# Writing the fp32r high part of h from PSUM on ScalarE, in a hybrid diffusion step on one Trainium2 core

## The chip, the core and the metric

The kernel runs on one core of one Trainium2 chip, as a single launch. The metric is the device time of one execution in microseconds (us); a run is given as the median of several executions. Engine names in the rows: PE is TensorE's matmul stream, PEld its weight loads, DVE is VectorE, ACT is ScalarE, POOL is GpSimd, SP is SyncE, which issues the DMAs.

## The reference

One step of a backbone over 2048 latent tokens and 128 prompt tokens, of width 1024. What bears on the change is the head of the layer: a root-mean-square norm, a scale and a shift per channel that come from the conditioning vector, and one combined projection whose columns feed four branches.

```python
def trunk_layer(x, cond, S0, ada_w, ada_b, norm_g, w_in, ...):
    mod = jax.nn.silu(cond) @ ada_w + ada_b
    shift, scale, gate = jnp.split(mod, 3, axis=-1)
    h = rmsnorm(x, norm_g) * (1 + scale[:, None]) + shift[:, None]
    p = h @ w_in
    qkv, g_a, beta_logit, a_logit, uv, g_b, x_c, g_c, x_d, g_d = jnp.split(p, _split_points(), axis=-1)
    y_a, S_new = deltanet_branch(qkv, g_a, beta_logit, a_logit, S0, conv_qkv, a_log, dt_bias, dn_norm_g)
    y_b = sgu_branch(uv, g_b, sgu_norm_g, sgu_w, sgu_b)
    y_c = pool_branch(x_c, g_c, pool_w, pool_scale)
    y_d = fourier_branch(x_d, g_d, fourier_w)
    out = jnp.concatenate([y_a, y_b, y_c, y_d], axis=-1) @ w_out
    return x + gate[:, None] * out, S_new
```

The first branch is a chunked gated delta rule: in chunks of 64 tokens it needs the inverse of a unit lower triangular matrix per chunk and head (`triangular_solve` in the reference), and then a scan over the chunks in both directions.

## The kernel before, in words

**Tiles and groups.** The latent tokens are 16 tiles of 128, the prompt is one more. They go through the first phase in three groups (`phase_a(gi)`, gi = 0, 1, 2). The transposed, modulated activations of one group stand in `hT`: the channels on the partitions, in 8 feature blocks f of 128 channels, the group's tokens on the free axis, 776 columns for groups 0 and 1 (six tiles and 8 columns of the next for the convolution), 640 for group 2. `hT` has one copy only. So a block of it may be written for the next group when the last projection of the old group has read it.

**Two parts of fp32.** The projections run in fp32r on TensorE, with each fp32 operand split in a high part (its rounding to fp32r) and a low part (the rest). `hT[0]` holds the high parts, `hT[1]` the low ones. `mm3` (L246 to L250) issues three matmuls for each feature block: high by high, high by low, low by high. Weights are loaded and split in the same way by `load_w` (L229 to L244): high part on ScalarE (L242) or, later in the program, on VectorE (L240), low part by a subtract on VectorE or GpSimd (L243).

**From x to hT.** `x_prep` loads tiles of x, adds the position embedding, and scales each token by its reciprocal root mean square (L331, in place). `x_fin` (L334) goes over the 8 feature blocks. For each: up to four TensorE transposes (L342) into one bank of PSUM `ps`; one ScalarE activation with the scale and bias of the block's channels, which writes the fp32 tile `h` (L344; four buffers, shared with another use under the tag "pr"); then `h_split`: VectorE's cast of `h` to fp32r, which is the high part (L353), and the subtract of the two, which is the low part (L354), on VectorE for even f and on GpSimd for odd f. Where `spill` is set, SyncE then stores `h` to DRAM (L348). The bank is one of two (`pa`) for the first half of group 0, taken in turn from `pc` and `pa` for its second half, and the single bank `pc` for groups 1 and 2. There are 56 such blocks: 24 of 384 columns, 16 of 392, and 16 of 128 (tile 15 and the prompt, in group 2).

**What follows in a group.** The first projection gives x_d and the delta-rule logits (272 columns per tile of tokens; matmuls at L250 named `pj<-BIG 128x272`; evicted by ScalarE into `xdt`, L923, and by VectorE into `lg`, L924). Then, for each of two pairs of heads, the convolution channels k, q and v are projected (chunks of 384 and 392 columns), convolved on VectorE (L832) and turned to token order. `pair_pre` builds the chunk matrices: key products (matmuls L660), decay factors (exp on ScalarE for Pd, Po and Pf, the last at L681), products on VectorE (Ld at L670, Po at L676, Pf at L692 with the matmuls L690). Pair 1's `pair_pre` of groups 0 and 1 is held back (`pend`) and runs after the next group's x_d projection. When both pairs are there, `lanes_solve` (L728, L730) inverts the triangular blocks step by step, VectorE and GpSimd each on its share of the rows; for group 0 it is cut into five pieces that are pulled in between other work, and groups 1 and 2 are solved together. Later come the scan, the Fourier branch, the other branches and the output projection with the residual (in the trace from about 1040 us on).

**What sets the order.** No order is written by hand. Each engine has one queue that runs in order; a scheduler fills the queues from the program's order, its priorities and its own estimate of when things are ready. So an edit in one place can move instructions on every engine. `x_prep` and `x_fin` run under one raised priority (`hp(OXv[0])`), `load_w` under another, and the projections' matmuls under none.

Of the kernel before, what the change touches and what calls it, by code (L numbers as in the profile page):

```python
# [9 lines left out]
F32 = mybir.dt.float32  # L10
# [3 lines left out]
AF = mybir.ActivationFunctionType  # L14
ALU = mybir.AluOpType
# [129 lines left out]
def tile_dit_step(ctx: ExitStack, tc: tile.TileContext, io: dict, dbg=None, stop=None):  # L145
    nc = tc.nc
# [53 lines left out]
    hT = [BIG[:, i * NH:(i + 1) * NH].rearrange("p (k t) -> p k t", k=KC) for i in range(2)]  # L200
# [6 lines left out]
    modab = cst.tile([128, 2, KC, 2], F32, name="modab")  # L207
# [5 lines left out]
    def hp(o):  # L213
        return tc.high_priority(offset=o)
# [119 lines left out]
    def x_fin(prep, fs=range(KC), pss=(pc,)):  # L334
        with hp(OXv[0]):
            tiles, off, spill, xts = prep
            w = sum(rows for _, rows in tiles)
            cond = 1 if tiles[0][0] == NTS else 0
            for f in fs:
                ps = pss[f % len(pss)]()  # L340
                for j, (i, rows) in enumerate(tiles):
                    nc.tensor.transpose(ps[:, j * 128:j * 128 + rows], xts[j][:rows, f * 128:(f + 1) * 128], ident[:rows, :rows])  # L342
                h = hp_.tile([128, 512], F32, tag="pr", name="h", bufs=4)
                nc.scalar.activation(h[:, :w], ps[:, :w], AF.Identity, scale=modab[:, 0, f, cond:cond + 1],  # L344
                                     bias=modab[:, 1, f, cond:cond + 1])
                h_split(h[:, :w], f, off)
                if spill is not None:
                    nc.sync.dma_start(out=h_d[spill, :, f, off:off + 384], in_=h[:, :384])  # L348

    def h_split(h, f, off):  # L350
        w = h.shape[1]
        hi = hT[0][:, f, off:off + w]
        nc.vector.tensor_copy(hi, h)  # L353
        (nc.gpsimd if f % 2 else nc.vector).tensor_tensor(hT[1][:, f, off:off + w], h, hi.bitcast(F32), op=ALU.subtract)  # L354

    def out_dbg(name, ap):
        if name in dbg:
# [4 lines left out]
    with tc.tile_pool(name="ada", bufs=3, reuse_waits="tile") as ada_p:  # L362
# [82 lines left out]
        with hp(300):  # L445
            mod_q(0, a0)
        a2 = ada_load(2)
        x_fin(p1, (0, 1), (pa,))
        with hp(300):
            mod_q(1, a1)  # L450
        a3 = ada_load(3)
        xd_k(range(3), 0)
        x_fin(p1, (2, 3), (pa,))
        with hp(300):
            mod_q(2, a2)
        xd_k(range(3), 1)
        x_fin(p1, (4, 5), (pa,))
        with hp(300):
            mod_q(3, a3)
# [866 lines left out]
    op = [ctx.enter_context(tc.tile_pool(name="opa_", bufs=1, side="right", reuse_waits="tile"))]  # L1326
# [110 lines left out]
```

## Time and profile before

| | |
|---|---|
| median of 3 runs | 1256.94 us (1252.34 to 1257.28) |
| the profiled execution | 1259.96 us |
| its span on the core | 1258.2 us |
| granted TensorE clock, mean | 0.917 |
| busy in the span: PE, DVE, ACT, POOL | 1100.5, 875.8, 414.3, 560.2 us |
| DMA | 204.21 MB, 162 GB/s mean |

The profiled execution is one program run, 1.8 us longer than its span, and 3.0 us above the median. Times in the rows below are us from the span's start. The busy shares are averages over stages that differ, so the rows are cut by stretch. The granted clock is the share of TensorE's full speed that was granted in the stretch; 1.00 is 2.4 GHz, and the lower level is 1.2 GHz.

### The profile page before, as it was taken

To read this page: it belongs to the slowest core of one execution; us is meant where nothing else is said; L and a number is where in the kernel's file an instruction comes from. 1 tells how busy PE (TensorE), PEld (TensorE's weight loads), DVE (VectorE), ACT (ScalarE), POOL (GpSimd) and SP (SyncE) were. 2 spreads that over 40 slices of the span, in tenths; PEclk is the share of its full clock that TensorE was granted. 3 is DMA by queue.
4 is the path that set the end of the run, shared out by engine and by line. 5 is a ranking of instruction groups with operands and counts; after the bars stand their busy time and mean duration, and the time that the engine had idled before them with its cause. 6 is when DMAs were issued, how large, how long until landed. Compare 5 with 4: busy or idle time off the path is not lost.

```text
span 1258.2 us, 28860 instructions
## 1 busy us (share of the span) xinstructions
PE 1100.5 (87%) x11635; PEld 998.4 (79%) x11635; DVE 875.8 (70%) x1864; ACT 414.3 (33%) x836; POOL 560.2 (45%) x551
## 2 busy tenths in 40 slices
PE   5798999986578899878997989999899979999997
PEld 2598888875566889774886878888889969999997
DVE  3768886999987477999577263584433378888665
ACT  2355765444344585310523102112111211111111
POOL 1347456799973154797040033223132543432212
PEclk9999988998766899798998989999999969999999
DMA  9978559543271558425245656767735555544331
GB/s 303 331 265 269 148 136 254 189 102 72 60 169 40 128 129 188 111 82 189 61 122 164 168 149 180 232 211 253 208 119 177 176 169 164 174 144 140 122 126 68
DMA packets 251388, 204.21 MB, mean 162 GB/s; under 512 B 109138, under 2 KB 218706, under 8 KB 250998
## 3 DMA queue, kind: packets, MB, share of 16 engines
q1 hardware_dynamic: 251254, 202.37, 55.1%
q8 instruction: 91, 1.49, 0.5%
q14 instruction: 43, 0.35, 0.1%
HBM read 138.86 MB, written 63.46 MB: 161 GB/s over the span
## 4 chain that ended last, share of the span: by engine, by line
PE 35%; DVE 8%; DMA 7%; POOL 5%; issue 3%; SPq 2%; ACT 1%; DVEq 0%; POOLq 0%; ACTq 0%
PE pj L250 28%; DMA wst<-in_wt_dram 3%; PE pa L1043 3%; POOL LL L730 2%; POOL ltmp L728 2%; DVE BIG L240 1%; DMA tab<-in_cdft_dram 1%; DVE X L752 1%; POOL BIG L243 1%; PE pb L1384 1%; PE pc L1043 1%; SPq L1034 1%; DMA ga<-ga_d 1%; DMA wos<-in_wo_dram 1%; DVE BIG L1207 1%
## 5 line engine op out<-in xcount | busy, mean ns | idle before, releaser
L250 PE MATMUL pj<-BIG 128*128 128x256 f32 (+4 forms) x3888 | 638.6, 320 | 34.0 <-DVE BIG L240 7.8
L250 PEld LDWEIGHTS pj<-BIG 128*128 128x128 f32 x3888 | 581.2, 201 | 54.9 <-issue 13.9
L250 PE MATMUL pj<-BIG,yh 128*128 128x256 f32 x1088 | 196.9, 287 | 5.7 <-ACT BIG L1346 4.7
L250 PEld LDWEIGHTS pj<-BIG,yh 128*128 128x128 f32 x1088 | 164.8, 191 | 8.8 <-ACT BIG L1346 5.1
L243 POOL TENSOR_TENSOR BIG<-wst,BIG 128x512 fp32r<-128x512 f32 (+1 forms) x66 | 94.7, 1436 | 171.9 <-DVE BIG L240 77.7
L250 PE MATMUL pj<-BIG,yl 128*128 128x256 f32 x544 | 141.9, 286 | 0.0
L250 PEld LDWEIGHTS pj<-BIG,yl 128*128 128x128 f32 x544 | 99.0, 191 | 0.7
L240 DVE CAST BIG<-wst 128x512 fp32r<-128x512 f32 (+2 forms) x72 | 44.9, 624 | 75.9 <-DMA wst<-in_wt_dram 41.5
L1404 POOL TENSOR_TENSOR z<-z,xs 128x1024 f32<-128x1024 f32 x16 | 40.2, 2510 | 72.5 <-DVE z L1396 62.0
L832 DVE SCALAR_TENSOR_TENSOR acc<-raw,prm,acc 128x768 f32<-128x768 f32 (+1 forms) x72 | 68.6, 976 | 4.8 <-ACT acc L830 4.8
L1050 POOL TENSOR_TENSOR gS<-S,sc_s 128x256 f32<-128x256 f32 x32 | 21.5, 672 | 97.3 <-DVE S L1065 85.4
L728 POOL TENSOR_TENSOR ltmp<-LL 64x60 f32<-64x60 f32 (+29 forms) x60 | 60.9, 1015 | 5.4 <-ACT LL L717 2.0
L730 POOL TENSOR_TENSOR LL<-LL,ltmp 64x60 f32<-64x60 f32 (+29 forms) x60 | 61.8, 1031 | 3.3
L1365 ACT ACTIVATE yh<-yt 128x768 fp32r<-128x768 f32 (+1 forms) x34 | 20.6, 628 | 125.2 <-issue 59.9
L243 DVE TENSOR_TENSOR BIG<-wst,BIG 128x512 fp32r<-128x512 f32 (+1 forms) x66 | 52.7, 799 | 10.7 <-ACT BIG L242 8.4
L354 POOL TENSOR_TENSOR BIG<-h,BIG 128x384 fp32r<-128x384 f32 (+2 forms) x28 | 32.7, 1167 | 61.6 <-DVE BIG L353 57.8
L730 DVE TENSOR_TENSOR LL<-LL,ltmp 64x60 f32<-64x60 f32 (+29 forms) x60 | 53.8, 896 | 1.1
L242 ACT ACTIVATE BIG<-wst 128x512 fp32r<-128x512 f32 (+1 forms) x60 | 37.6, 633 | 51.1 <-DMA wst<-in_wt_dram 29.4
L728 DVE TENSOR_TENSOR ltmp<-LL 64x60 f32<-64x60 f32 (+29 forms) x60 | 53.2, 887 | 1.3
L1061 ACT ACTIVATE xn<-pa 128x256 f32<-128x256 f32 x34 | 13.0, 381 | 106.9 <-PE pa L1043 106.9
L1212 ACT ACTIVATE g<-pj 128x256 f32<-128x256 f32 (+1 forms) x64 | 22.6, 398 | 70.5 <-PE pj L250 61.3
L1396 DVE TENSOR_TENSOR z<-pj,gbc 128x256 f32<-128x256 f32 x68 | 26.1, 421 | 28.2 <-PE pj L250 27.9
(292 smaller groups left out, 1921.9 us busy)
## 6 DMA issues: line engine op xcount, KB each, us to landing
wst<-in_wt_dram SPq DMA_DIRECT2D x96, 256.0 KB
R<-rec_d SPq DMA_DIRECT2D x136, 128.0 KB
ada<-in_ada_dram SPq DMA_DIRECT2D x24, 512.0 KB
C<-com_d SPq DMA_DIRECT2D x68, 128.0 KB
xs<-xs_d SPq DMA_DIRECT2D x16, 512.0 KB
out_dram<-z SPq DMA_DIRECT2D x16, 512.0 KB
x<-in_xs_dram SPq DMA_DIRECT2D x13, 512.0 KB
xs_d<-x SPq DMA_DIRECT2D x13, 512.0 KB
```

The source lines that it names most:

```text
L240: nc.vector.tensor_copy(hi[:, ks, a:a + w], st[:, :, :w])
L242: nc.scalar.activation(hi[:, ks, a:a + w], st[:, :, :w], AF.Copy)
L243: (nc.vector if k0 == 0 else nc.gpsimd).tensor_tensor(lo[:, ks, a:a + w], st[:, :, :w], hi[:, ks, a:a + w].bitcast(F32), op=ALU.subtract)
L250: nc.tensor.matmul(out, lh[a](k), rh[b](k), start=(k == first and i == 0), stop=(k == last and i == 2))
L354: (nc.gpsimd if f % 2 else nc.vector).tensor_tensor(hT[1][:, f, off:off + w], h, hi.bitcast(F32), op=ALU.subtract)
L728: eng.tensor_tensor(tv, X[:, bs, j, j + 1:32].unsqueeze(2).to_broadcast([n, nb, j, ni]), bc(X[:, bs, 0:j, j], ni), op=ALU.mult)
L730: eng.tensor_tensor(X[:, bs, 0:j, j + 1:32], X[:, bs, 0:j, j + 1:32], tv, op=ALU.add)
L832: nc.vector.scalar_tensor_tensor(o, raw[:, si + j:si + j + n], w[:, j:j + 1], o, op0=ALU.mult, op1=ALU.add)
L1043: nc.tensor.matmul(ps[o, q], lh(q)[hp], rh[hp, q])
L1212: [lambda a, w, ps, t=t: nc.scalar.activation(t[:, a:a + w], ps[:, :w], func) for t in ts])
L1396: nc.vector.tensor_tensor(z[:, ns], ps, gbc[:, cd, ns], op=ALU.mult)
L1404: nc.gpsimd.tensor_tensor(z, z, xs, op=ALU.add)
```

## The change

`h_split` is gone. Behind the activation that writes `h`, ScalarE runs a second activation with the same scale and bias on the same bank of PSUM, and writes the fp32r high part straight into `hT[0]` (L347 of the changed kernel). The subtract is in line (L349) and reads `h` and the high part as before, on the same engines as before. 56 VectorE casts go, 56 ScalarE activations come, and two of ScalarE's table loads go; the other instructions are the same in number. Lines after L354 are two lower in the changed kernel (L681 becomes L679, L728 becomes L726).

```diff
--- before.py
+++ after.py
@@ -343,15 +343,13 @@
                 h = hp_.tile([128, 512], F32, tag="pr", name="h", bufs=4)
                 nc.scalar.activation(h[:, :w], ps[:, :w], AF.Identity, scale=modab[:, 0, f, cond:cond + 1],
                                      bias=modab[:, 1, f, cond:cond + 1])
-                h_split(h[:, :w], f, off)
+                hi = hT[0][:, f, off:off + w]
+                nc.scalar.activation(hi, ps[:, :w], AF.Identity, scale=modab[:, 0, f, cond:cond + 1],
+                                     bias=modab[:, 1, f, cond:cond + 1])
+                (nc.gpsimd if f % 2 else nc.vector).tensor_tensor(hT[1][:, f, off:off + w], h[:, :w], hi.bitcast(F32),
+                                                                  op=ALU.subtract)
                 if spill is not None:
                     nc.sync.dma_start(out=h_d[spill, :, f, off:off + 384], in_=h[:, :384])
-
-    def h_split(h, f, off):
-        w = h.shape[1]
-        hi = hT[0][:, f, off:off + w]
-        nc.vector.tensor_copy(hi, h)
-        (nc.gpsimd if f % 2 else nc.vector).tensor_tensor(hT[1][:, f, off:off + w], h, hi.bitcast(F32), op=ALU.subtract)
 
     def out_dbg(name, ap):
         if name in dbg:
```

The order moves in three places that matter here. The first is **ScalarE**, from the second half of group 1's `x_fin` (blocks of 392 columns) to the exp of Pf of group 0's pair 1. Before:

```order
L834 ACT_TABLE_LOAD
L834 ACTIVATE acc<-acc 128x768
L344 ACTIVATE h<-pc,modab 128x392
L242 ACTIVATE BIG<-wst 128x4x136
L242 ACTIVATE BIG<-wst 128x4x128
L344 ACTIVATE h<-pc,modab 128x392
L923 ACTIVATE xdt<-pj 128x256 x3
L681 ACT_TABLE_LOAD
L681 ACTIVATE Pf<-Pf 128x1536
L708 ACTIVATE tm<-pb 128x2x256
```

And now:

```order
L344 ACTIVATE h<-pc,modab 128x392
L347 ACTIVATE BIG<-pc,modab 128x392
L242 ACTIVATE BIG<-wst 128x4x128
L679 ACT_TABLE_LOAD
L679 ACTIVATE Pf<-Pf 128x1536
L344 ACTIVATE h<-pc,modab 128x392
L347 ACTIVATE BIG<-pc,modab 128x392
L706 ACTIVATE tm<-pb 128x2x256
L706 ACTIVATE tm<-pb 128x2x128
L921 ACTIVATE xdt<-pj 128x256
L344 ACTIVATE h<-pc,modab 128x392
L347 ACTIVATE BIG<-pc,modab 128x392
```

Before, the exp of Pf stood behind the last of the eight h's; now it stands ahead of six of the eight pairs of activations, which are strewn among the projection's evictions.

The second is **VectorE** behind the projection of group 1 (the copies of lg), through the products of group 0's pair 1 (Ld, Po, Pf) to the first steps of its solve (L728 and L730, now L726 and L728). Before:

```order
L538 TENSOR_TENSOR gl<-lg,prm 128x48
L533 TENSOR_SCALAR bl<-bl 128x48
L535 RECIPROCAL be_1821<-bl 128x6x2x2 x2
L559 TENSOR_SCALAR bmx_1826<-be_1821,cm 128x24
L542 SCALAR_TENSOR_TENSOR gl<-gl,t_2348 128x48
L543 TENSOR_TENSOR gl<-gl,nal 128x48
L670 TENSOR_TENSOR Ld<-Pd,pb 128x192 x4
L676 TENSOR_TENSOR Po<-Po,pb 128x192 x2
L692 TENSOR_TENSOR Pf<-Pf,pb 128x384 x2
L243 TENSOR_TENSOR BIG<-wst,BIG 128x4x128
L692 TENSOR_TENSOR Pf<-Pf,pb 128x384 x2
L728 TENSOR_TENSOR ltmp<-LL 64x60
```

And now:

```order
L690 TENSOR_TENSOR Pf<-Pf,pb 128x384 x2
L726 TENSOR_TENSOR ltmp<-LL 64x60
L728 TENSOR_TENSOR LL<-LL,ltmp 64x2x30
L726 TENSOR_TENSOR ltmp<-LL 64x116
L728 TENSOR_TENSOR LL<-LL,ltmp 64x2x2x29
L922 COPY lg<-pj 128x16
L726 TENSOR_TENSOR ltmp<-LL 64x168
L922 COPY lg<-pj 128x16
L728 TENSOR_TENSOR LL<-LL,ltmp 64x2x3x28
L726 TENSOR_TENSOR ltmp<-LL 64x216
L728 TENSOR_TENSOR LL<-LL,ltmp 64x2x4x27
L922 COPY lg<-pj 128x16
```

Before, the first row shown reads lg, and all its copies stood ahead of that row, so ahead of the products and the solve; now the last three copies stand behind the first solve steps.

The third is **TensorE** in the same stretch: transposes (L342), the projection with 272 columns (L250), and the key products of group 0's pair 1 (L660 before, L658 now). Before:

```order
L342 MATMUL pc<-cm,xb 128x128 x3
L342 MATMUL pc<-cm,x 128x8
L574 MATMUL pb<-S_744,cm 64x3x6
L573 MATMUL pb<-S_744,cm 64x12 x2
L574 MATMUL pb<-S_744,cm 64x3x6 x2
L573 MATMUL pb<-S_744,cm 64x12 x2
L574 MATMUL pb<-S_744,cm 64x3x6
L250 MATMUL pj<-BIG 128x272 x3
L629 MATMUL pb<-cm,acc 128x128 x6
L250 MATMUL pj<-BIG 128x272 x105
L660 MATMUL pb<-sl 32x64 x48
```

And now:

```order
L250 MATMUL pj<-BIG 128x272 x12
L342 MATMUL pc<-cm,xb 128x128 x3
L342 MATMUL pc<-cm,x 128x8
L250 MATMUL pj<-BIG 128x272 x3
L658 MATMUL pb<-sl 32x64 x16
L250 MATMUL pj<-BIG 128x272 x9
L658 MATMUL pb<-sl 32x64 x9
L342 MATMUL pc<-cm,xb 128x128 x3
L342 MATMUL pc<-cm,x 128x8
L250 MATMUL pj<-BIG 128x272 x24
L658 MATMUL pb<-sl 32x64 x4
L250 MATMUL pj<-BIG 128x272
```

Before, the key products stood behind one block of 105 projection matmuls, and the transposes ahead of all of it; now the three are mixed in pieces.

## Rows read from the trace of the kernel before

**Rows 1.** The page's first part: each engine's busy time, its share of the span, and its number of instructions.

```profile
PE 1100.5 (87%) x11635; PEld 998.4 (79%) x11635; DVE 875.8 (70%) x1864; ACT 414.3 (33%) x836; POOL 560.2 (45%) x551
```

**Rows 2.** The instructions of line L353 over the whole span: shortest, median and longest in ns, first and last start; and, from the same answer, the line on who waited for them.

```profile
L353 DVE CAST BIG<-h x56: 209/358/3812, 47.1 to 420.2; 128x384 fp32r<-128x384 f32 x24, 128x392 fp32r<-128x392 f32 x16, 128x128 fp32r<-128x128 f32 x16
...
  POOL BIG L354: 57.8, 20
```

**Rows 3.** Busy time in windows of 20 us. Columns: window, its length, then busy time and number of instructions of PE, PEld, DVE, ACT and POOL, the granted TensorE clock, the DMA share and GB/s. The last line sums six windows, from 240 to 360.

```profile
300.00:320.00 20.00, 15.21 (x88) 13.87 (x88) 20.00 (x20) 10.61 (x13) 19.28 (x13) 0.83 0.36 75
320.00:340.00 20.00, 12.05 (x144) 11.11 (x144) 19.90 (x28) 7.70 (x14) 19.46 (x15) 0.81 0.20 40
340.00:360.00 20.00, 12.51 (x104) 11.98 (x105) 20.00 (x29) 8.40 (x14) 18.00 (x17) 0.59 0.61 146
sum 120.00, PE 85.97 PEld 80.88 DVE 119.47 ACT 49.43 POOL 109.71; mean PE 14.33 PEld 13.48 DVE 19.91 ACT 8.24 POOL 18.29
```

**Rows 4.** The same columns, for the three windows before those.

```profile
180.00:200.00 20.00, 16.27 (x113) 13.59 (x112) 15.00 (x37) 15.60 (x27) 8.68 (x9) 0.81 1.02 243
200.00:220.00 20.00, 20.00 (x223) 19.61 (x223) 10.48 (x19) 10.75 (x20) 14.32 (x13) 0.93 0.92 257
220.00:240.00 20.00, 17.07 (x146) 16.02 (x145) 17.96 (x31) 12.12 (x23) 18.64 (x22) 1.00 0.79 248
```

**Rows 5.** The same columns, for two long stretches.

```profile
340.00:420.00 80.00, 63.97 (x487) 54.43 (x488) 60.85 (x139) 36.60 (x82) 40.97 (x52) 0.64 0.46 106
1040.00:1240.00 200.00, 199.89 (x2356) 192.88 (x2355) 154.99 (x447) 37.67 (x68) 63.54 (x56) 1.00 0.43 141
```

**Rows 6.** Busy time of the casts alone (L353 on DVE) by stretch: window, its length, busy time and number, the granted clock, DMA share, GB/s. The sum is over five windows, of which two are left out.

```profile
0.00:100.00 100.00, 6.85 (x16) 0.97 0.92 305
...
300.00:345.00 45.00, 8.14 (x7) 0.79 0.31 69
345.00:425.00 80.00, 7.16 (x17) 0.67 0.43 99
sum 425.00, DVE 31.07; mean DVE 6.21
```

**Rows 7.** Groups by line and shape: line, engine, operation, output and input, count, then busy time, mean ns of one, and the idle time of the engine before them.

```profile
L344 ACT ACTIVATE h<-pc,modab 128x384 f32<-128x384 f32 x16 | 10.8, 676 | 16.0 <-PE pc L342 9.9 <-DVE BIG L354 4.1 <-issue 1.9
...
L344 ACT ACTIVATE h<-pc,modab 128x128 f32<-128x128 f32 x16 | 7.2, 453 | 8.6 <-PE pc L342 8.5
```

**Rows 8.** VectorE's timeline, three pieces: start, duration, line, operation; in brackets the idle time before it and what ended it.

```profile
154.39 0.35 DVE L353 CAST BIG<-h 128x384 fp32r<-128x384 f32 x1
...
308.42 1.54 DVE L353 CAST BIG<-h 128x384 fp32r<-128x384 f32 x2
...
310.43 3.81 DVE L353 CAST BIG<-h 128x384 fp32r<-128x384 f32 x1
...
316.73 5.77 DVE L354 TENSOR_TENSOR BIG<-h,BIG 128x384 fp32r<-128x384 f32 x1
...
350.12 0.34 DVE L353 CAST BIG<-h 128x384 fp32r<-128x384 f32 x1
```

**Rows 9.** ScalarE's timeline, three pieces, the same columns.

```profile
135.75 0.73 ACT L344 ACTIVATE h<-pc,modab 128x384 f32<-128x384 f32 x1
...
290.42 0.65 ACT L344 ACTIVATE h<-pc,modab 128x384 f32<-128x384 f32 x1
...
335.24 0.67 ACT L344 ACTIVATE h<-pc,modab 128x384 f32<-128x384 f32 x1 [0.27 <-PE pc L342]
```

**Rows 10.** VectorE's timeline between the two parts above.

```profile
204.86 0.17 DVE L924 COPY lg<-pj 128x16 f32<-128x16 f32 x1 [3.21 <-ACT xdt L923]
...
221.04 1.14 DVE L670 TENSOR_TENSOR Ld<-Pd,pb 128x192 f32<-128x192 f32 x4
...
228.01 0.38 DVE L728 TENSOR_TENSOR ltmp<-LL 64x60 f32<-64x60 f32 x1
```

**Rows 11.** TensorE's timeline in the same stretch.

```profile
199.10 15.29 PE L250 MATMUL pj<-BIG 128*128 128x272 f32 x105
214.32 1.44 PE L660 MATMUL pb<-sl 64*32 64x64 f32 x96
```

**Rows 12.** ScalarE's timeline in the same stretch.

```profile
195.98 0.68 ACT L344 ACTIVATE h<-pc,modab 128x392 f32<-128x392 f32 x1 [0.18 <-issue]
...
205.62 1.28 ACT L681 ACT_TABLE_LOAD   x1
206.92 1.49 ACT L681 ACTIVATE Pf<-Pf 128x1536 f32<-128x1536 f32 x1
```

**Rows 13.** The waits in 280 to 425: engine and line that waited <- what ended it: us in total, times, the longest.

```profile
PE pb L690 <- DVE Po L676: 7.6, 1, 7.6
...
PEld pc L342 <- ACT h L344: 5.0, 4, 2.4
...
ACT h L344 <- DVE BIG L354: 4.1, 1, 4.1
...
PE pj L250 <- DVE BIG L243: 3.6, 1, 3.6
```

**Rows 14.** The same view for 40 to 90.

```profile
PEld pa L342 <- ACT h L344: 3.4, 3, 2.7
...
PEld pj L250 <- DVE BIG L354: 1.3, 1, 1.3
```


## The prediction

> **What bounds the kernel now.** I read the totals first, then the busy times in windows of 20 us, then what waits in the windows where TensorE isn't full. In the totals [rows 1] the reader is to see that no engine fills the span: TensorE's matmuls are busy 87% of it, VectorE 70%, ScalarE 33%, GpSimd 45%. An average says nothing here, so the stages come next. From 1040 on TensorE is full, 199.89 of 200 us [rows 5]: what is gained earlier is carried to the end there, and so is what is lost. The changed lines run only up to 420 us [rows 2], so the question is what 0 to 420 gives.
>
> There, one stretch stands out: from 240 to 360 VectorE is busy 119.47 of 120 us, GpSimd 109.71, TensorE 85.97 and ScalarE 49.43 [rows 3]. In it VectorE and GpSimd solve group 0's lanes together (the pairs at L728 and L730), and VectorE is the bound. Before it, in 180 to 240, VectorE is busy 15.00, 10.48 and 17.96 us of each 20 [rows 4], so 16.6 us idle: it waits for the inputs of that solve. Behind it, 340 to 420, TensorE is busy 63.97 of 80 us at a mean granted clock of 0.64 [rows 5], so partly at the lower of its two levels, 1.2 GHz instead of 2.4.
>
> **What the change removes.** 56 VectorE casts (L353), of 0.21 to 3.81 us, median 0.36 [rows 2], together 31.07 us by stage [rows 6]. They cost very different amounts, and the stretch that counts is the full one: seven casts in 300 to 345, 8.14 us [rows 6], and one of 0.34 at 350 [rows 8], 8.5 us in all; eight undisturbed ones at the median would be 2.9.
>
> **Term A, casts out of the full stretch: −4.** The cast at 310 took 3.81 us, and the subtract behind it at 316, which has the same partner on GpSimd, 5.77 [rows 8], while GpSimd was busy 19.28 of 20 [rows 3]. So the long ones are not long by their own work: 0.34 is that of the cast at 350 [rows 8]. If the time over that is a hold-up by GpSimd, part of it moves to the next VectorE instruction when the cast is gone. The ends are −8.5 (all of it goes) and −2.9 (only the undisturbed durations go); I take −4, nearer the lower, since in the same rows the subtract, which stays, is held up longest.
> The Trainium skill ("SBUF — State Buffer", Who interferes with whom) speaks against taking the whole 8.5: a copy or cast that uses both port pairs excludes GpSimd, the later one blocks fully, and a tensor_tensor with two inputs in SBUF contends with GpSimd's reads too, so the solve's multiplications and the subtract would inherit the block. By it A would be −2.9; by the rows' plain sum −8.5. No run here shows yet which.
>
> **Term B, the solve starts earlier: −7.** This is what the order moves, not the cast. Before, the multiplications of pair 1 of group 0 (L660) stand on TensorE at 214.32, behind 105 projection matmuls with 272 columns in one block of 15.29 us [rows 11]; VectorE multiplies by them at 221.04 (L670) and the solve starts at 228.01 [rows 10]. In the changed order the L660 matmuls stand in pieces among those projection matmuls, and on VectorE the first solve step stands ahead of the last three copies of lg. VectorE has the room for it: before the first lg copy alone it waits 3.21 us for the projection's eviction [rows 10], and 16.6 us in sum [rows 4]. The ends are −15.3 (the whole block is passed) and 0 (the pieces still wait for the hi blocks, or GpSimd's share of the solve keeps the pace); I take half, −7, since the pieces are strewn through the block evenly.
>
> **Term C, the bank and ScalarE's queue: +4.** Before, ScalarE read the bank once (0.676 us for 128x384, 0.453 for 128x128 [rows 7]), and up to four h tiles ran ahead of hT, which has one copy and is free only when the old group's projections have read it: in group 1 an h was written at 135.75, in group 2 one at 290.42 [rows 9], and the first casts of the two came at 154.39 and 308.42 [rows 8]. Now the second activation has to wait for hT itself, holds the one pc bank while it waits, and blocks what is behind it in ScalarE's queue. In group 1's second part the order also puts the exp of Pf (1.49 us, behind a table load of 1.28 [rows 12]) ahead of six of the eight pairs; before, all eight h's were begun by 195.98, and the exp came at 206.92 [rows 12]. Transposes waiting for the bank: 5.0 us in 280 to 425 [rows 13]. Added activations of 24 blocks of 384 columns: 24 × 0.676 = 16.2 us at most, and 0 if all lies beside other work. Against a large sum speaks the last block of group 2's first part: its h was written at 335.24 [rows 9] and cast at 350.12 [rows 8], late in VectorE's queue, where ScalarE would now write it at once. That is no gain of its own: TensorE's projection waits until 351.14 for the weights' L243 (3.6 us [rows 13]). I take +4, a quarter of the 16.2: ScalarE is idle for more than half of the full stretch [rows 3], but one bank serves groups 1 and 2.
> One rule of the Trainium skill speaks against the change as such ("ScalarE: Activation LUTs", Rules for kernel authors): copies and additions belong on VectorE, which is faster per element. The rows agree on the price, 0.676 us against a median of 0.36; it would turn the sum only where ScalarE is the bound, and with 49.43 of 120 us it isn't.
>
> **Term D, 0 to 100: 0.** Group 0's 16 blocks have more than one bank (pa has two, and the second half takes turns between pc and pa); transposes wait there for h for 3.4 us [rows 14]. Ends: +3.4 (as much again) and −1.3 (a projection waits 1.3 us for the subtract behind a cast [rows 14]). GpSimd waits 57.8 us for casts in all [rows 2], which is worth nothing where GpSimd isn't the bound.
>
> **Term E, the 16 blocks of 128x128: 0.** 345 to 425 has 17 casts, 7.16 us [rows 6]; in their place come 16 × 0.453 = 7.2 us of ScalarE [rows 7]. The ends are −7.2 and +7.2; VectorE and ScalarE both have room there, so neither is taken.
>
> **Term F, the clock: −1.** At full clock the 63.97 us of 340 to 420 would be 63.97 × 0.64 = 41 us [rows 5], so 23 at most. The clock is low because TensorE stood idle in 320 to 360 (24.56 of 40 busy, the granted clock 0.81 and then 0.59 [rows 3]), waiting for VectorE: for L676 once 7.6 us [rows 13]. An earlier solve would shorten this a little. Ends −23 and 0.
>
> Two of ScalarE's table loads go too (1.28 us each [rows 12]); they lie in its free time: 0. The spill's DMA issues and GpSimd's subtracts are the same in number; only their place moves with h, which was ready early.
>
> **Sum:** −4 −7 +4 +0 +0 −1 = −8 against the profiled execution's 1259.96, so 1252. That execution was 3 us above the median of the runs, 1256.94, so the prediction is **1249**.
>
> **The rivals.**
> R1, slower: ScalarE's queue becomes the wait. Place: x_fin of groups 1 and 2. A second activation that waits for hT's block (the last reader of the old group is a projection matmul) stops the conv and projection evictions behind it, and TensorE waits for free pj banks. Price: C is +11 (two thirds of the 16.2), A −4, B 0, since the pair 1 work waits as well: +7, 1264. It decides from the point where the waits for the bank grow from 5.0 us [rows 13] past about 13. For it: one bank, and hT free 18 us after the first h of group 2 [rows 8, 9]. Against it: ScalarE waited 4.1 us for a free h at one place only [rows 13].
> R2, no difference: GpSimd's half of the solve holds the pace. It is busy 109.71 of 120 us [rows 3], so VectorE's casts were in its shadow; VectorE would just wait. A and B come to about −4 and C takes it back: 1257.
> R3, much faster: the clock comes back. If TensorE is kept busy through 320 to 360, half of the 23 us return, F is −11 in place of −1: 1239.
> That the change does not do what it says is out: the order of the changed kernel shows no cast at that line on VectorE and an activation behind every h on ScalarE.
>
> **How the numbers follow.** The forecast of 1249 gets 0.40 and R3 0.10: together 0.50 for faster. R2 gets 0.26, R1 0.24. A difference of 0.5%, 6.3 us, is about the smallest that a measurement of this kernel tells from none. The range: the low end is R3's 1239 with A at −8.5 and some 2 us more of B, 1233; the high end is R1's 1264 with A at −2.9 and nearly 1 more of C, 1266. Beyond these lie the ends of B, E and F together below, and all of the 16.2 of C, or E's end with R1, above. The forecast's own range, with A to −8.5 and −2.9 and B from −11 to −3, is 1241 to 1254.
>
> **What would show it.** Right: VectorE's idle time in 180 to 240 falls under 10 us, the first L726 on VectorE starts before 224, and the full stretch ends 8 to 12 us earlier; the subtracts there are still longer than 0.5 us; TensorE's part from 1040 on has the same length and starts earlier. Wrong: transposes that wait over 13 us for the bank in 280 to 425, conv evictions on ScalarE behind a waiting activation, or a solve that starts at the same time. A difference that first appears after 420, where nothing was changed but the order, would mean that the reordering decides and not the cast.

## The result, and the profile after

The changed kernel took 1267.62 us, median of 4 runs (1266.74 to 1272.80), against 1257.11 for the kernel before: 10.5 us slower by the medians, whose quotient is 1.0084. The ratio of the runs, 1.0131 with a 95% interval of 1.0093 to 1.0168, is larger; it isn't the quotient of these medians, and the same holds for the ratios below. Measured again beside the experiments the change was 1.0117 (1.0082 to 1.0153), 15 us by its medians. The forecast was 1249.

The page of the changed kernel, its first part, beside [rows 1]:

```profile
PE 1106.2 (87%) x11635; PEld 999.2 (79%) x11635; DVE 848.0 (67%) x1808; ACT 439.6 (35%) x890; POOL 547.1 (43%) x551
```

The work moved as planned: VectorE is 27.8 us less busy than before (875.8 to 848.0), ScalarE 25.3 us more, the counts are 56 fewer and 54 more. But the span grew by 12.8 us (1258.2 to 1271.0).

**What came out as hoped: VectorE's share of group 0's solve, but not the solve.** Timelines of the changed kernel: VectorE's first step of the solve, the last copy of lg, one of the convolution's multiply-adds and the last step of VectorE's share; then the last step of GpSimd's share (POOL), and the first of TensorE's transposes that read the solved blocks (L754, before L756):

```profile
225.28 0.21 DVE L726 TENSOR_TENSOR ltmp<-LL 64x60 f32<-64x60 f32 x1 [0.19 <-ACT LL L715]
...
231.45 0.16 DVE L922 COPY lg<-pj 128x16 f32<-128x16 f32 x1
...
334.01 6.05 DVE L830 SCALAR_TENSOR_TENSOR acc<-raw,prm,acc 128x768 f32<-128x768 f32 x1
...
344.16 0.26 DVE L728 TENSOR_TENSOR LL<-LL,ltmp 64x60 f32<-64x60 f32 x1
...
373.54 0.34 POOL L728 TENSOR_TENSOR LL<-LL,ltmp 64x60 f32<-64x60 f32 x1
...
375.68 1.19 PE L754 MATMUL pa<-cm,LL 48*128 48x48 f32 x16
```

And the last three of these before:

```profile
366.70 0.25 DVE L730 TENSOR_TENSOR LL<-LL,ltmp 64x60 f32<-64x60 f32 x1
...
368.26 0.34 POOL L730 TENSOR_TENSOR LL<-LL,ltmp 64x60 f32<-64x60 f32 x1
...
370.96 1.08 PE L756 MATMUL pa<-cm,LL 48*128 48x48 f32 x8
```

VectorE's share starts at 225.28, 2.7 us earlier than before [rows 10], and ends at 344.4 instead of 366.9, so VectorE is rid of it 22 us sooner. GpSimd's share ends at 373.9 instead of 368.6. The transposes read the blocks of both engines, and start at 375.68 instead of 370.96. So the solve as a whole ended 5 us later: GpSimd's share set its end. In 225 to 375 GpSimd is busy 124.54 us instead of 136.69, so it waits more there.

The subtracts of VectorE in 300 to 345 took 8.25 us before and take 1.09 now, but there are two of them instead of four; the other two come later (lines L354 before and L349 now, by stage; columns as in [rows 6], with GpSimd's busy time behind VectorE's):

```profile
300.00:345.00 45.00, 8.25 (x4) 4.12 (x3) 0.79 0.31 69
```

```profile
300.00:345.00 45.00, 1.09 (x2) 0.99 (x1) 0.77 0.25 56
```

Long instructions didn't vanish with the casts, though: others are long now, as the L830 above with 6.05 us, whose like elsewhere take about 1.0. It has two inputs in SBUF, and GpSimd was working on tiles in SBUF all the while. That fits what the Trainium skill says ("SBUF — State Buffer", Who interferes with whom): a VectorE instruction with two inputs in SBUF contends with a GpSimd instruction that reads SBUF. The trace shows the durations; that GpSimd makes them is argued.

**Where the time went: x_fin.** ScalarE's timeline of the changed kernel, group 1's blocks (h is L344, the high part L347):

```profile
123.37 0.67 ACT L344 ACTIVATE h<-pc,modab 128x384 f32<-128x384 f32 x1 [3.76 <-PE pc L342]
...
155.91 0.65 ACT L347 ACTIVATE BIG<-pc,modab 128x384 fp32r<-128x384 f32 x1
157.70 0.67 ACT L344 ACTIVATE h<-pc,modab 128x384 f32<-128x384 f32 x1 [1.13 <-PE pc L342]
158.27 0.67 ACT L347 ACTIVATE BIG<-pc,modab 128x384 fp32r<-128x384 f32 x1
...
187.23 0.66 ACT L344 ACTIVATE h<-pc,modab 128x384 f32<-128x384 f32 x1
...
202.51 1.49 ACT L679 ACTIVATE Pf<-Pf 128x1536 f32<-128x1536 f32 x1 [3.32 <-DVE Pf L678]
...
221.82 0.66 ACT L344 ACTIVATE h<-pc,modab 128x392 f32<-128x392 f32 x1
```

Block 0's h is written at 123.37; its high part at 155.91, near the 154.39 of VectorE's first cast before [rows 8]. For these 32 us the bank is held, and block 1's transposes, h and high part begin only at 157. Before, h ran ahead, one of them written at 135.75 [rows 9]. From 157 on the blocks of the changed kernel come one by one, each with its transposes, two activations and the way between the engines, until 221.82; before, the last h stood at 195.98 [rows 12]. The exp of Pf stands among them, at 202.51 and so earlier than the 206.92 of before.

In group 2 the first h came at 278.02 before, and 17 us later, at 295.36, in the changed kernel:

```profile
278.02 0.70 ACT L344 ACTIVATE h<-pc,modab 128x384 f32<-128x384 f32 x1
```

What hangs on x_fin is the x_d projection, on TensorE. Its last matmuls in group 1 and in group 2, in the changed kernel:

```profile
224.81 1.37 PE L250 MATMUL pj<-BIG 128*128 128x272 f32 x9
...
434.91 1.07 PE L250 MATMUL pj<-BIG 128*128 128x272 f32 x6
```

And the last in group 2 before:

```profile
421.30 1.08 PE L250 MATMUL pj<-BIG 128*128 128x272 f32 x6
```

In both rows of group 2 only the first three matmuls have 272 columns; the ends given here and in the table below are those of the last matmul with 272 columns. In group 1 the projection ends at 226.2 instead of 214.4 (behind [rows 11]), 11.8 us later; in group 2 at 435.6 instead of 421.9. From there to the end of the span it is 836.3 us before and 835.4 now. So the loss stood at 12 us by 226 and at nearly 14 by 436, all of the span's 12.8, and what VectorE saved between lay beside the path. That the delay of group 1 is simply carried on is not shown: e4 below ends its group 2 projection almost as before.

Part of the 11.8 us is the clock: in 155 to 190 TensorE is busy 27.42 of 35 us at a granted clock of 0.77, before 30.88 at 0.90; it stood idle more, and ran slower where it ran. The windows of the changed kernel (columns as in [rows 3]):

```profile
180.00:200.00 20.00, 13.33 (x94) 11.63 (x93) 14.85 (x23) 18.51 (x31) 10.12 (x11) 0.74 0.81 202
200.00:220.00 20.00, 18.72 (x224) 16.32 (x224) 9.21 (x24) 10.87 (x19) 10.24 (x10) 1.00 0.68 179
220.00:240.00 20.00, 14.47 (x120) 13.27 (x118) 18.32 (x28) 11.83 (x24) 16.44 (x20) 0.97 0.84 242
...
358.00:432.00 74.00, 65.67 (x553) 55.31 (x549) 45.73 (x106) 41.99 (x101) 29.50 (x44) 0.63 0.45 104
1040.00:1240.00 200.00, 198.65 (x2338) 191.12 (x2339) 150.97 (x468) 36.83 (x67) 62.63 (x55) 0.99 0.43 138
```

VectorE's 180 to 240 shows 17.6 us of idle time, no less than the 16.6 of [rows 4], and TensorE in 180 to 240 has 46.52 us of work instead of 53.34. ScalarE is busy 18.51 us of 180 to 200, where it was 15.60 [rows 4], so its queue may hold blocks up there as well. The group 2 projection (358 to 432 holds most of it) runs at a clock of 0.63 (0.64 in [rows 5]). From 1040 on TensorE is full as before.

The waits in 280 to 425, as [rows 13]:

```profile
POOL BIG L349 <- ACT BIG L347: 24.6, 5, 7.1
...
PEld pc L342 <- ACT BIG L347: 4.7, 3, 3.8
```

The same view for 100 to 230, where group 1's loss was made, before:

```profile
POOL BIG L354 <- DVE BIG L353: 6.8, 6, 2.3
...
PEld pc L342 <- ACT h L344: 5.0, 5, 1.7
```

And now:

```profile
POOL BIG L349 <- ACT BIG L347: 21.7, 5, 7.9
DVE BIG L349 <- ACT BIG L347: 11.3, 4, 5.9
...
PEld pc L342 <- ACT BIG L347: 5.9, 2, 3.6
```

Transposes that wait for the bank: 4.7 us instead of 5.0 in 280 to 425, and 5.9 instead of 5.0 in 100 to 230. The sign that the prediction named for its slower rival, over 13 us of such waits, is absent, and the rival's time came all the same. In TensorE's order the transposes stand behind other work, so the delay of a block shows as order. In 100 to 230 it also shows as subtracts that wait for the high part: GpSimd's 21.7 us instead of 6.8, and VectorE's 11.3. (In 280 to 425 GpSimd's 24.6 us are no sign: it waited 27.9 there for VectorE's casts before.)

### The profile page after: what moved, and what is told of

Read it like the earlier page. It is cut to its first block, busy times and chain, and to the rows that moved or that the text cites. A ratio compares the mean times of both kernels' runs of the same rounds, so it can differ in the third digit from the quotient of the medians.

```text
span 1271.0 us, 28878 instructions
## 1 busy us (share of the span) xinstructions
PE 1106.2 (87%) x11635; PEld 999.2 (79%) x11635; DVE 848.0 (67%) x1808; ACT 439.6 (35%) x890; POOL 547.1 (43%) x551
## 4 chain that ended last, share of the span: by engine, by line
PE 40%; DVE 18%; DMA 10%; POOL 7%; issue 4%; ACT 4%; SPq 2%; DVEq 0%; POOLq 0%; ACTq 0%
PE pj L250 30%; PE pa L1041 3%; DMA wst<-in_wt_dram 2%; DVE acc L830 2%; DVE LL L728 2%; DVE ltmp L726 2%; POOL ltmp L726 2%; POOL LL L728 2%; POOL BIG L243 1%; DVE BIG L243 1%; DMA R<-rec_d 1%; DMA raw_d<-yd 1%; PE pa L754 1%; DVE BIG L240 1%; PE pb L658 1%
## 5 line engine op out<-in xcount | busy, mean ns | idle before, releaser
L250 PE MATMUL pj<-BIG 128*128 128x256 f32 (+4 forms) x3888 | 644.3, 321 | 37.9 <-DVE BIG L240 10.4
L250 PEld LDWEIGHTS pj<-BIG 128*128 128x128 f32 x3888 | 583.3, 201 | 60.8 <-issue 18.4
L250 PE MATMUL pj<-BIG,yh 128*128 128x256 f32 x1088 | 197.1, 286 | 4.2 <-DVE BIG L1345 1.6
L250 PEld LDWEIGHTS pj<-BIG,yh 128*128 128x128 f32 x1088 | 164.1, 190 | 8.0 <-ACT BIG L1344 1.8
L243 POOL TENSOR_TENSOR BIG<-wst,BIG 128x512 fp32r<-128x512 f32 (+1 forms) x66 | 99.4, 1507 | 157.8 <-DVE BIG L240 78.6
L250 PE MATMUL pj<-BIG,yl 128*128 128x256 f32 x544 | 140.0, 283 | 0.0
L250 PEld LDWEIGHTS pj<-BIG,yl 128*128 128x128 f32 x544 | 98.3, 190 | 0.3
L830 DVE SCALAR_TENSOR_TENSOR acc<-raw,prm,acc 128x768 f32<-128x768 f32 (+1 forms) x72 | 70.8, 1005 | 9.8 <-ACT acc L828 9.6
L243 DVE TENSOR_TENSOR BIG<-wst,BIG 128x512 fp32r<-128x512 f32 (+1 forms) x66 | 56.4, 855 | 18.2 <-ACT BIG L242 16.2
L726 POOL TENSOR_TENSOR ltmp<-LL 64x60 f32<-64x60 f32 (+29 forms) x60 | 65.9, 1098 | 5.5 <-ACT LL L715 2.5
L349 POOL TENSOR_TENSOR BIG<-h,BIG 128x384 fp32r<-128x384 f32 (+2 forms) x28 | 27.6, 985 | 83.5 <-ACT BIG L347 83.5
L728 POOL TENSOR_TENSOR LL<-LL,ltmp 64x60 f32<-64x60 f32 (+29 forms) x60 | 59.9, 998 | 3.4
L728 DVE TENSOR_TENSOR LL<-LL,ltmp 64x60 f32<-64x60 f32 (+29 forms) x60 | 56.9, 948 | 1.3
L726 DVE TENSOR_TENSOR ltmp<-LL 64x60 f32<-64x60 f32 (+29 forms) x60 | 53.6, 894 | 1.8 <-ACT LL L715 0.2
L1364 DVE TENSOR_TENSOR yl<-yt,yh 128x768 fp32r<-128x768 f32 (+1 forms) x34 | 41.3, 1231 | 10.3 <-ACT yh L1363 10.3
```

Of the source, the lines that this page charges most:

```text
L243: (nc.vector if k0 == 0 else nc.gpsimd).tensor_tensor(lo[:, ks, a:a + w], st[:, :, :w], hi[:, ks, a:a + w].bitcast(F32), op=ALU.subtract)
L250: nc.tensor.matmul(out, lh[a](k), rh[b](k), start=(k == first and i == 0), stop=(k == last and i == 2))
L726: eng.tensor_tensor(tv, X[:, bs, j, j + 1:32].unsqueeze(2).to_broadcast([n, nb, j, ni]), bc(X[:, bs, 0:j, j], ni), op=ALU.mult)
L728: eng.tensor_tensor(X[:, bs, 0:j, j + 1:32], X[:, bs, 0:j, j + 1:32], tv, op=ALU.add)
L830: nc.vector.scalar_tensor_tensor(o, raw[:, si + j:si + j + n], w[:, j:j + 1], o, op0=ALU.mult, op1=ALU.add)
L1364: nc.vector.tensor_tensor(yl[:, q], yt[:, q], yh[:, q].bitcast(F32), op=ALU.subtract)
```

## The experiments

Theory 1: the second read holds the only bank until hT is free, so h can't run ahead. Theory 2: ScalarE's 25 us more are the price. Theory 3: the scheduler's new order moves the time by chance. All ratios are against the kernel before on the same chip. The ends of the x_d projections, the clock in 370 to 420 and the span are from each one's profile.

| kernel | ratio (95%) | x_d of group 1 ends | of group 2 | clock 370 to 420 | span |
|---|---|---|---|---|---|
| before | 1 | 214.4 | 421.9 | 0.62 | 1258.2 |
| change | 1.0131 (1.0093 to 1.0168) | 226.2 | 435.6 | 0.59 | 1271.0 |
| e9, the change again | 1.0117 (1.0082 to 1.0153) | 227.9 | 432.5 | 0.66 | 1272.4 |
| e1, ScalarE from h | 1.0033 (0.9996 to 1.0070) | 220.4 | 418.4 | 0.80 | 1254.7 |
| e2, VectorE from PSUM | 1.0082 (1.0044 to 1.0120) | 228.6 | 436.2 | 0.60 | 1261.8 |
| e3, change with three banks | 1.0135 (1.0076 to 1.0194) | 212.3 | 435.4 | 0.67 | 1266.4 |
| e4, change in group 1 | 1.0038 (1.0006 to 1.0069) | 225.7 | 423.0 | 0.76 | 1261.9 |
| e5, change in group 2 | 1.0082 (1.0039 to 1.0124) | 216.5 | 423.0 | 0.57 | 1264.6 |
| e6, change in group 0 | 0.9990 (0.9964 to 1.0016) | 206.1 | 408.0 | 0.72 | 1241.9 |
| e7, change in groups 1, 2 | 1.0046 (1.0025 to 1.0068) | 226.3 | 425.0 | 0.75 | 1255.0 |
| e8, 8 casts twice | 1.0054 (1.0022 to 1.0086) | 211.4 | 415.5 | 0.76 | 1253.9 |
| e10, one h tile | 1.0279 (1.0244 to 1.0314) | 245.3 | 444.1 | 0.66 | 1286.1 |
| e11, 8 casts to ScalarE, from h | 0.9858 (0.9831 to 0.9885) | 214.5 | 403.9 | 0.93 | 1235.2 |
| e12, the same from PSUM | 1.0010 (0.9978 to 1.0043) | 217.1 | 423.7 | 0.62 | 1253.1 |
| e13, e11 and VectorE's casts too | 1.0042 (1.0006 to 1.0077) | 217.5 | 423.9 | 0.63 | 1262.4 |
| e14, e11 and the change in group 1 | 1.0101 (1.0041 to 1.0161) | 224.7 | 424.6 | 0.73 | 1258.2 |
| e15, e11 and the change in group 0 | 0.9940 (0.9904 to 0.9975) | 211.1 | 404.6 | 0.82 | 1241.4 |

The span less the end of group 2's x_d projection is 825 to 842 us in all of them, while that end itself moves by 40: the large differences are made in the stretch up to it. The small ones need not be: in e2 it ends 14 us later than before with a span only 3.6 longer, in e5 1 us later with a span 6.4 longer. The kernel before was spread over 1244 to 1263 us in these sessions, so a single profile, as that of e6, can lie well off its median; the ratios carry the verdicts.

**Holding the bank against ScalarE's load (e1, e2).** The edit in the changed kernel's second activation (e1), and in its place (e2):

```diff
-                nc.scalar.activation(hi, ps[:, :w], AF.Identity, scale=..., bias=...)
+                nc.scalar.activation(hi, h[:, :w], AF.Copy)                          # e1
+                nc.vector.tensor_scalar(hi, ps[:, :w], scale, bias, ...)             # e2: mult, add
```

> The high part is written by ScalarE as in the change, but from the fp32 h in SBUF, so the PSUM bank is free after the first activation and h can run ahead of hT again. Theory 1 (the bank is held until hT is free, three transposes run ahead less in group 1): the x_d projection of group 1 ends near 214 us again instead of 225, total 1250 to 1260. Theory 2 (ScalarE's added 25 us in its queue is the price): no better than the changed kernel, 1264 to 1270. Theory 3 (only the reordering): anywhere between.

> The high part is written by VectorE, not by ScalarE, but straight from the PSUM bank with the same scale and bias, so the bank is held until hT is free while ScalarE has no more work than in the kernel before. Theory 1: as slow as the changed kernel or slower, 1264 to 1275, first h's of group 1 no longer ahead. Theory 2: as the kernel before, 1252 to 1260.

Measured +0.33% and +0.82%. Reading h in place of the bank takes most of the loss away with ScalarE nearly as busy (435.6 us, in the change 439.6); holding the bank brings more than half of it with none of ScalarE's added work, and with VectorE as busy as before (876.3 against 875.8). Theory 1 holds for the larger part. That theory 2 has a part isn't excluded: e1's interval reaches 1.007, and its group 1 projection ended at 220.4, 6 us later than before, where 214 was expected.

**More banks (e3).** `pss=(pc,)` became `pss=(pc, pa)`.

> The changed kernel with the transposes of groups 1 and 2 taking turns between the bank pc and the two banks pa, as group 0's second half does. Theory 1: three h's can be ahead of hT again, about 8 of the 11 us lost by 225 us come back, total 1254 to 1262, unless other users of pa (the lanes' transposes) are held up. Theory 2: 1264 to 1270.

Measured +1.35%, against theory 1, at first sight. Group 1 did get its time back: its x_d ends at 212.3. But `pa` also serves the lanes' output, and ScalarE's second h of group 2 came at 395.10 after a first at 275.53: the new order put group 2's blocks behind other work. The test isn't clean.

**By group (e4 to e7).** The second activation stands under `if`, with VectorE's cast of h in the other groups.

> The change in group 1 alone (16 blocks); groups 0 and 2 keep VectorE's cast. Theory 1: group 1 carries all of the loss, 1265 to 1272, with the x_d projection of group 1 ending about 10 us later than before. Theory 2: 16 of 56 activations, 29% of the loss, 1259 to 1261.

> The change in group 2 alone (8 blocks of 384 and 16 of 128 columns). Theory 1a (group 2's x_fin alone carries the loss, since in it the end of the x_d projection, 422 us before and 432 after, is what the rest follows): 1262 to 1268 against 1255 or so, +0.6 to +1.1%. Theory 1b (a delay of either group alone is absorbed by slack in group 2, as that of group 1 was, and only both together show): within 0.4%.

> The change in group 0 alone, where the blocks have three banks and hT is free. All theories of the bank: within 0.4% of before. Theory 3 (the reordering alone moves the time by a per cent): anything from -1 to +1.3%.

> The change in groups 1 and 2, VectorE's cast in group 0. Theories 1a and 1b: all of the loss, +0.9 to +1.4%, the x_d projection of group 1 ending near 226 us and that of group 2 near 432. If group 0 has a part in it: under +0.8%.

Measured +0.38, +0.82, −0.10 and +0.46%. The expectation for e4 failed: group 1's projection did end 11 us later (225.7), but group 2's at 423.0, 1 us later than before. So group 2 absorbed the delay of group 1 there; in e14 below it did not. Group 2 alone costs more, as theory 1a had it (group 2's own blocks carry the loss), but not by its mechanism: its x_d projection ended 1 us later than before, so the loss lies behind it. Group 0, with its three banks and a free hT, costs nothing. That groups 1 and 2 together cost less than the whole change, and not more than group 2 alone, failed the expectation for e7 and is not explained: the parts don't add up.

**VectorE's casts twice (e8).** In the kernel before, `h_split` issues its cast two times for the 8 blocks of 384 columns of group 2.

> The kernel before, with each cast of group 2's first part (8 blocks of 384 columns, in the stretch where VectorE is full) issued twice: some 4 to 8 us more of VectorE there. If that stretch's VectorE sets the end, as the prediction's term A took it: +4 to +8 us (+0.3 to +0.7%). If the solve's end is not waited for: within 0.2%.

Measured +0.54% (2.8 to 10.8 us). VectorE's time in its full stretch does count, as term A had it, if the order that moved with the edit has no part in it.

**The change again, and one h tile (e9, e10).** e9 has no edit. In e10, the kernel before:

```diff
-        pr = (pool or hp_).tile([128, 512], F32, tag="pr", name="pr", bufs=5 if pool else 4)
+        pr = (pool or hp_).tile([128, 512], F32, tag="pr", name="pr", bufs=5 if pool else 3)
 ...
-                h = hp_.tile([128, 512], F32, tag="pr", name="h", bufs=4)
+                h = hp_.tile([128, 512], F32, tag="h1" if tiles[0][0] >= 6 else "pr", name="h", bufs=1 if tiles[0][0] >= 6 else 3)
```

> The change itself, unaltered, on the chip of the experiments. Theory 4 (two prices that add: holding the bank, as in the kernel with VectorE reading PSUM, +0.8%, and ScalarE's second pass, as in the kernel that casts h on ScalarE, +0.3%): +0.8 to +1.3%. If the first measurement was high by chance: near the kernel with the change in groups 1 and 2, +0.2 to +0.7%.

> The kernel before with one h tile of its own for groups 1 and 2, in place of four shared ones (position rows keep three of four): VectorE casts, ScalarE as before, the bank is given back at once, but h can't run ahead of hT. If the lost run ahead is what holding the bank costs: +0.5 to +1.0%, the first h's of group 1 from 155 us on. If it is something else about reading PSUM twice: within 0.3%.

e9: +1.17%, near the sum of e1 and e2 (0.33 and 0.82), as theory 4 has it. e10: +2.79%, more than expected. ScalarE's timeline of e10, the first three blocks of group 1 and the last:

```profile
122.17 0.67 ACT L344 ACTIVATE h<-pc,modab 128x384 f32<-128x384 f32 x1
...
162.86 0.65 ACT L344 ACTIVATE h<-pc,modab 128x384 f32<-128x384 f32 x1
165.88 0.67 ACT L344 ACTIVATE h<-pc,modab 128x384 f32<-128x384 f32 x1 [2.37 <-POOL BIG L354]
...
241.67 0.68 ACT L344 ACTIVATE h<-pc,modab 128x392 f32<-128x392 f32 x1 [6.50 <-DMA h_d<-h]
```

Block 0 at 122, block 1 only at 163, the last at 241.67, and the projection ends at 245.3, 31 us late. No bank is held here and no engine has more to do, so a lost run ahead is enough for a loss. Its size isn't that of the change: the one tile also waits for its subtract and for the store of h (6.50 us at the last), and the position rows and group 0 share three buffers instead of four.

**Eight casts to ScalarE, from h, and from PSUM (e11, e12, e13).** Only the first part of group 2 is changed, the 8 casts of VectorE's full stretch:

```diff
+                if tiles[0][0] == 12:
+                    nc.scalar.activation(hi, h[:, :w], AF.Copy)                                     # e11
+                    nc.scalar.activation(hi, ps[:, :w], AF.Identity, scale=..., bias=...)           # e12, in its place
+                    nc.vector.tensor_copy(hT[1][:, f, off:off + w], h[:, :w])                       # e13, beside e11's
+                else:
+                    nc.vector.tensor_copy(hi, h[:, :w])
```

> The kernel before, with only the 8 casts that stand where VectorE is full (first part of group 2) moved to ScalarE, which reads h in SBUF, so nothing holds the bank. By term A of the prediction, and by the kernel with these casts twice (+0.5%): -0.2 to -0.6%. If the casts' time there is not waited for: within 0.2%.

> As the kernel that moves 8 casts to ScalarE (-1.4%), but those 8 high parts are written from the PSUM bank, as in the change. The two differ in one operand. Theory 5 (ScalarE off VectorE's full stretch gains, holding the one bank costs more): the gain is lost, -0.3 to +0.8%, and h of the second to eighth block no longer written before 320 us. If reading PSUM twice costs nothing: -1.1 to -1.7%.

> ScalarE writes the 8 high parts from h as in the kernel that gained 1.4%, and VectorE still casts h, into the slot of the low part that the subtract then overwrites; so VectorE has its 8 casts again. If VectorE's time in its full stretch is the gain: back to -0.3 to +0.3%. If the gain is the reordering, or that the high part is there earlier: -1.0 to -1.5%.

e11 gained 1.42%, more than expected, and beats both kernels: 1236.95 us, median of 5. e12, which differs in what the high part is read from (the bank, with scale and bias, in place of h), gains nothing (+0.10%). ScalarE's timeline of e11, the first four h's, the first high part, and the eighth h with its high part:

```profile
277.24 0.70 ACT L344 ACTIVATE h<-pc,modab 128x384 f32<-128x384 f32 x1
...
289.79 0.65 ACT L344 ACTIVATE h<-pc,modab 128x384 f32<-128x384 f32 x1
...
292.30 0.67 ACT L344 ACTIVATE h<-pc,modab 128x384 f32<-128x384 f32 x1 [1.25 <-PE pc L342]
...
300.45 0.67 ACT L344 ACTIVATE h<-pc,modab 128x384 f32<-128x384 f32 x1
...
306.92 0.51 ACT L348 ACTIVATE BIG<-h 128x384 fp32r<-128x384 f32 x1
...
334.81 0.67 ACT L344 ACTIVATE h<-pc,modab 128x384 f32<-128x384 f32 x1 [0.25 <-PE pc L342]
335.51 0.53 ACT L348 ACTIVATE BIG<-h 128x384 fp32r<-128x384 f32 x1
```

And of e12, the first two blocks and the eighth h:

```profile
279.03 0.72 ACT L344 ACTIVATE h<-pc,modab 128x384 f32<-128x384 f32 x1
...
310.07 0.65 ACT L348 ACTIVATE BIG<-pc,modab 128x384 fp32r<-128x384 f32 x1
...
313.73 0.67 ACT L344 ACTIVATE h<-pc,modab 128x384 f32<-128x384 f32 x1
314.30 0.66 ACT L348 ACTIVATE BIG<-pc,modab 128x384 fp32r<-128x384 f32 x1
...
363.88 0.66 ACT L344 ACTIVATE h<-pc,modab 128x384 f32<-128x384 f32 x1
```

In e11 four h's stand before the first high part, and the eighth is at 334.81. In e12 the bank is held from 279 to 310, and the eighth h comes at 363.88, 29 us later; only the source of the read differs, and the order that follows from it. This pair shows theory 1 in one place.

e1 moves the same 8 casts in the same way, and the other 48 with them, and gains nothing (+0.33%). So these 48, or the order that moved with them, cost some 1.8% although no bank is held; no run tells these apart.

e13 gives VectorE its 8 casts back and loses the gain too (+0.42%): the high part being there early isn't what gained, VectorE's time is, unless the order of e13 has a part. How 8 casts make 17 us is seen in the windows of e11, e12 and e13, 345 to 370 and 370 to 420:

```profile
345.00:370.00 25.00, 16.71 (x97) 14.44 (x95) 24.93 (x54) 15.56 (x29) 22.34 (x35) 0.66 0.75 171
370.00:420.00 50.00, 47.43 (x517) 42.01 (x517) 34.59 (x90) 30.59 (x77) 17.60 (x21) 0.93 0.43 106
```

```profile
345.00:370.00 25.00, 20.67 (x155) 19.18 (x156) 21.33 (x39) 16.95 (x29) 16.47 (x30) 0.72 0.72 171
370.00:420.00 50.00, 44.35 (x335) 35.57 (x334) 33.44 (x93) 21.49 (x57) 16.43 (x18) 0.62 0.35 75
```

```profile
345.00:370.00 25.00, 16.96 (x136) 15.57 (x136) 24.81 (x46) 14.31 (x26) 22.58 (x33) 0.71 0.63 149
370.00:420.00 50.00, 41.22 (x328) 33.09 (x329) 34.45 (x94) 20.75 (x53) 17.27 (x21) 0.63 0.41 92
```

In 345 to 370 the three run at much the same clock. In 370 to 420 the granted clock is 0.93 in e11, 0.62 and 0.63 in the others, 0.62 in the kernel before: with 47.43 us busy TensorE does 44 us' worth at full clock, in e12 44.35 × 0.62 = 27. The kernel before has two idle times of TensorE there (2.4 us for L765's XE and 2.6 for x, at 382.6 and 388.4), e12 of 1.4 and 2.1, e13 of 5.5 and 1.1, and with them windows of 10 us at 0.50 to 0.71 in 370 to 410, partly at the lower level of 1.2 GHz; e11 has nothing over 1 us between 367 and 420. That the clock is what stretches 8 casts to 17 us is read from these rows, not shown by a run of its own.

**Groups 1 and 0 on top of e11 (e14, e15).**

> Group 2's 8 blocks from h on ScalarE, group 1's 16 blocks from PSUM as in the change. If the 11 us that group 1's x_d projection ends later are still hidden in group 2, as in the kernel with the change in group 1 alone (+0.4%): -0.8 to -1.4%. If they come through now that group 2 is shorter: -0.5 to +0.2%.

> Group 2's 8 blocks from h on ScalarE, group 0's 16 blocks from PSUM (three banks, hT free). Group 0's part was worth -0.1% alone: -1.3 to -1.7%.

e14: +1.01%, outside both expected ranges (by the medians of 1262.03 and 1254.83 it is +0.57%). With group 1 from PSUM the whole gain of e11 goes, and more: its 10 us no longer hide, and the clock is 0.73. e15: −0.60%, less than e11 and than expected though group 0 alone cost nothing. Its solve starts at 253.7 instead of 227.5, so the order changed far from the edit; but e6's starts late too, at 249.4, and costs nothing. Why e15 loses 0.8% against e11 stays open; theory 3 may have a part of this size.

These two runs show something else. In e6 and e15 the solve ends at 389.6 and 390.6, some 21 us later than before, with −0.10% and −0.60%: the time doesn't follow the end of the solve.

## Why the prediction was wrong, step by step

- **Term C failed by its size.** It was put at +4, a quarter of ScalarE's added 16.2 us. The mechanism was named (the second activation waits for hT and holds the one bank), but priced as the second pass, where the price is that blocks no longer run ahead: 11.8 us at the end of group 1's projection, and e11 against e12 some 1.5% in group 2's 8 blocks alone. The run ahead was also read too short: the first h of group 2 was written at 278.02, 30 us before the first cast, not 18.
- **Term B failed by its path.** VectorE's share of the solve started 2.7 us earlier, not 7: the key products stand among blocks that now come later, and VectorE's idle time in 180 to 240 didn't fall. And an earlier start was counted as time gained, us for us. VectorE was taken for the bound of the solve, but GpSimd's share ended last before (368.6 against 366.9) and does now (373.9 against 344.4), and e6 and e15 show that the time doesn't follow the end of the solve at all.
- **Term A bought nothing in the change.** VectorE was rid of the casts and of its share of the solve, but GpSimd's share ended later, and TensorE came to the same place 12 us late from group 1. Without the bank held, the 8 casts of the full stretch alone are worth 17 us (e11), where the prediction had 4: by the rows of 370 to 420, because the clock comes back with them. That casts in this stretch count at all fits e8 and e13.
- **The rule of the Trainium skill on the two engines** ("ScalarE: Activation LUTs", Rules for kernel authors) sends additions and multiplications to VectorE as faster per element; its row doesn't name copies, as the prediction has it. For the price of one the trace agrees, and for the change as a whole its advice came out right. e11 goes against it, and gains, where VectorE is full and ScalarE isn't.
- **Term D** held: group 0 alone moves nothing (e6). **Term E** likely didn't: e5 and e12 differ in the 16 blocks of 128x128 alone, and stand at +0.82% and +0.10%, some 9 us for E instead of 0. Why, no run shows.
- **Term F and R3**: the clock didn't come back in the change (0.63 in 358 to 432). It did in e11, as R3 described.
- **R1 came near in time** (1264 forecast, 1268 measured, its chance 0.24): one bank, x_fin of groups 1 and 2, B worth nothing, C some +11. Part of that is luck, since its −4 for A was not there. Its place on the path was wrong: not evictions and pj banks, but the projection's start. And its sign, waits for the bank past 13 us, was wrong: 4.7.
- **R2 had the solve right**: GpSimd's share set its end, and what VectorE saved there was worth nothing. Its time (1257) missed, since it let C only take back A and B.

## What to carry to other kernels

When a cast is moved to read the PSUM bank directly, ask when its destination is free: a reader that has to wait for it holds the bank, and with one bank the whole chain of transposes stops running ahead. Move the work to the idle engine where the other is full, and let it read the copy in SBUF, as e11 does; e1, which did so everywhere, gained nothing. Price a lost run ahead by the round trip of a block times the blocks that were ahead, not by the busy time of the instruction that was added. As an estimate here: from 157.70 to 221.82 the changed kernel wrote an h every 4.6 us, and three more were ahead before, so 14 us, against 11.8 measured. Look for the loss in when blocks start, since in queues with other work it need not show as a wait of the engine that makes the blocks. And where two engines share a piece of work, read the end of both shares before counting what one of them saves.

## What the runs showed of the hardware

ScalarE's copy of 128x384 took 0.51 us from SBUF (e11, L348) and 0.66 from PSUM (the change, L347). An undisturbed cast on VectorE takes 0.34 [rows 8], but VectorE's instructions last up to 6 us beside a busy GpSimd, so in e11 the slower engine was the cheaper place. A difference that no theory here explains (e15 against e11, 0.8%) and a granted clock between 0.57 and 0.93 in the same stretch (370 to 420) were as large as most terms of the sum.
